# A two-block transformer on one core: the router's dependent chain runs without GpSimd beside it, and the overflow branch, the second gather, half of the list weights and the transposed lists move into later expert pairs

## The chip, the cores and the metric

The kernel runs on one core of a Trainium2 chip. A core has TensorE (matrix multiplies; PE in the rows, its weight loads PEld), VectorE (DVE), ScalarE (ACT), GpSimd (POOL) and SyncE (SP), which here only issues transfers. Each engine works through its own list of instructions in order; they meet at semaphores. All five share 16 DMA engines, which bring weights from the large memory (HBM) into the on-chip memory. The metric is device time of one execution in microseconds, smaller is better.

## The reference, cut to what matters

The program is two blocks on 256 tokens of width 1024. The change touches the mixture of experts that ends each of the two layers of the first block:

```python
def grouped_moe(x, router_w, router_bias, w_gate, w_up, w_down):
    scores = softmax(x @ router_w)                       # 16 experts in 4 groups
    biased = scores + router_bias
    # the best group by the sum of its two best biased scores; in it, the two best experts
    weights = sel / sum(sel)                             # of the two chosen scores
    combine = sum(one_hot(expert_idx, 16) * weights[..., None], axis=1)
    y = 0
    for e in range(16):
        he = silu(x @ w_gate[e]) * (x @ w_up[e])         # 1024 -> 512
        y = y + combine[:, e:e+1] * (he @ w_down[e])     # 512 -> 1024
    return y
x = layer_norm(ALPHA * x + grouped_moe(x), g, b)
```

Everything is float32, so one layer's experts hold 96 MB of weights in units of 1 MiB (1.049 MB): 16 experts by three matrices of 2 MiB.

## The kernel before, in words

The tokens stand as two tiles of 128 rows (index t). Ahead of a layer's experts, `add_ln_router` finishes a projection, adds it to the residual, normalizes it to `tt` and multiplies it with the router's weights, so that the logits `lg` come from TensorE while the second token tile is still being normalized. `zh` and `zl` are `tt` split in a rounded high part and the rest (`split`), as the operands of the gathers.

`route` then runs a chain of some forty small VectorE instructions (128x32 and smaller): softmax with an exact exponential, ranks, chosen groups, the selection `esel`, and, after five small matmuls that count positions (`pos`, `tot`), the position of each token in its expert's list (`posm`). Each expert has 64 slots. `Pm[h]` is a 0/1 matrix from tokens to slots for half h of the experts (h = 0: pairs 0 to 3; h = 1: pairs 4 to 7); `comb` holds the weights of the chosen experts. `ofint` says whether an expert got more than 64 tokens; if so, `overflow` does the rest in a branch on every engine. In the profiled run no engine enters it. `gather_half(h, ks)` multiplies `zh`, `zl` with `Pm[h]` and lets ScalarE put the result into the tiles `xg`, the experts' inputs.

`moe` goes over eight pairs of experts, two experts side by side in the 128 columns. Pair p: gate matmuls (`first(p, "gate")`, out `pg`), the transposed hidden state of the pair before, one half of the scatter of the pair before that (`back`, out `sct`), up matmuls (`pu`), silu and product (`gated`), the other half of the scatter, and the down matmuls of the pair before (`down`, out `po`). A pair takes 12 units of weights, 4 for each matrix. In pair 0 stand also the second gather, the weights of the lists turned to slots (`pc`, copied to `cg`), and the transposed lists `PT` (`PmT`), which the scatters need.

The weights of the whole program are one list, `order`; `Stream` loads it in that order from SyncE's queue. How far ahead it may load is the number of places that `W.spare` names by kind: `w` (tiles that elsewhere hold split weights), `big`, `x`, `q`, besides three `raw` tiles. A place is free again when TensorE has read its unit; SyncE waits for that in order, unit by unit. A transfer also waits for the transfer eight before it. The kernel is written in program order by hand (nothing reorders it). `ada_go` and `ada_end` put small pieces of the second block's modulation between.

In SyncE's list the end of the branch carries waits for all eight of its transfer semaphores: where they hold on the way past as well, every transfer issued before must have landed ere the next is issued. The other engines' lists carry there a wait for their own earlier work.

Of the kernel before, what the change touches and what calls it, by code (L numbers as in the profile page):

```python
# [213 lines left out]
def _build(nc, tc, A, out, ctx, order, plan):  # L214
# [266 lines left out]
    def add_ln_router(l, x_old, wname, xh, xl, nm):  # L481
# [32 lines left out]

        def rest():
            unit(1)
            for t in range(2):
                G.tensor_sub(zl[:, t], tt[:, t], zh[:, t].bitcast(F32))
            for t in range(2):
                for i, op in enumerate((OP.mult, OP.add)):  # L520
                    G.tensor_tensor(tt[:, t], tt[:, t], gb[:, i], op=op)

# [481 lines left out]
    def route(l, x):  # L1004

        tt, zh, zl, lg, rest = x
# [70 lines left out]
        def weights():  # L1077
            comb, cd = sm(32, "comb"), sm(2, "cd")
            V.tensor_tensor(comb, sc, eself, op=OP.mult)
            V.tensor_reduce(cd, r3(comb), axis=AX, op=OP.add)  # L1080
            V.reciprocal(cd, cd)
            V.tensor_tensor(r3(comb), r3(comb), b16(cd), op=OP.mult)
            return comb
# [11 lines left out]
        gather_half(0, range(8))  # L1095
        return xg, gather_half, Pm, comb, tt

# [50 lines left out]

    def beyond(l, pair, half, px, first, tt, zh, zl, P2, PT2, x2, o2, h2, ps, p, ps_, cg2):

        V.tensor_scalar_add(ps_, px[:, :2], -float(first))
        for t in range(2):
            V.tensor_scalar(P2[:, t], iota, ps_[:, t:t + 1], None, op0=OP.is_equal)
        f2 = x2[:, 0].rearrange("p (k n) -> p k n", k=8)
        for k in range(8):
# [29 lines left out]
        for nh in range(2):  # L1185
            c = slice(nh * 512, nh * 512 + 512)
            split(o2[:, 0, c], o2[:, 1, c], ps[2 + nh])
        for t in range(2):
            for nh in range(2):
                c = slice(nh * 512, nh * 512 + 512)  # L1190
                for i in range(2):
                    T.matmul(ps[nh], PT2[:, t], o2[:, i, c], start=i == 0, stop=i == 1)
                V.tensor_add(tt[:, t, c], tt[:, t, c], ps[nh])

    def moe(l, x, hooks):

# [30 lines left out]

        W.spare.update(big=1)
        for p in range(9):
            if p == 4:  # L1230
                W.spare["big"] = 3
# [5 lines left out]
            if p == 0:  # L1237
                gather_half(1, range(4), "BB")
                pc = mm([128, 128], "pc", "B")
                for q in range(8):  # L1240
                    for t in range(2):
                        T.matmul(pc[:, 16 * q:16 * q + 16], Pm[q // 4][:, t, 128 * (q % 4):128 * (q % 4) + 128].bitcast(F32),
                                 comb[:, 16 * t:16 * t + 16], start=t == 0, stop=t == 1)
                cg = cp.tile([128, 8], F32, name=f"cg{l}")
                for s in range(2):
                    V.tensor_copy(cg[64 * s:64 * s + 64], pc[64 * s:64 * s + 64, s:s + 127:18])
            else:
# [940 lines left out]
```

## Time and profile before

| | |
|---|---|
| time, three runs | 1975.96, 1968.2, 1970.99 us (median 1970.99) |
| the profiled execution | 1969.34 us, span from the first to the last instruction 1967.5 us |
| TensorE busy | 1839.5 us, 93% |
| VectorE / ScalarE / GpSimd busy | 984.3 / 706.3 / 392.3 us |
| transfers | 424.23 MB, mean 216 GB/s over the span |

TensorE's busy share is high everywhere, since matmuls overlap and their ends are modelled; it does not say that TensorE sets the time. The two expert stages lie at about 238 to 478 us and 696 to 938 us. In most of each the transfer rate stands at 422 GB/s.

### The profile page before, as it was taken

Reading aid. Unit: us, or ns where it says so; the run is one execution under the profiler, and the core shown is the slowest. Engines: PE = TensorE matmul, PEld = TensorE weight load, DVE = VectorE, ACT = ScalarE, POOL = GpSimd, SP = SyncE. Lnnn points to the kernel's source line nnn. Section 1 sums busy time; section 2 is a strip of 40 time slices with the busy share of each in tenths; the row PEclk is TensorE's granted clock in tenths of the full one; section 3 lists DMA queues with packets and bytes.
Section 4 is the critical chain, followed back from the end, with each engine's and each line's share of the span. In section 5 each row is a group of like instructions: output and inputs, shape, how many; then the busy total and the mean of one; then the engine's idle time right before and its main releaser. Section 6 shows DMA issues by size and latency. Waiting matters only on the chain.

```text
span 1967.5 us, 25607 instructions
## 1 busy us (share of the span) xinstructions
PE 1839.5 (93%) x10038; PEld 1332.9 (68%) x10038; DVE 984.3 (50%) x1717; ACT 706.3 (36%) x1214; POOL 392.3 (20%) x604
## 2 busy tenths in 40 slices
PE   8999699999999789999889989899999998999999
PEld 6888443334788553333678877688888886669998
DVE  6884601113785611112755666734353446756665
ACT  6654220002454331111454553522222225545442
POOL 0012200003334300020565673200000005410000
PEclk9999799999999889999999999999999999899999
DMA  7555679999756759999621221423333422455552
GB/s 260 203 207 201 235 278 421 422 423 423 285 193 219 273 198 408 422 422 423 249 108 66 86 65 65 135 102 130 105 129 107 136 87 65 181 220 197 186 181 106
DMA packets 81300, 424.23 MB, mean 216 GB/s; under 512 B 9376, under 2 KB 9824, under 8 KB 48656
## 3 DMA queue, kind: packets, MB, share of 16 engines
q1 hardware_dynamic: 78480, 409.66, 55.3%
q0 software_dynamic: 2688, 12.81, 1.8%
q8 instruction: 83, 1.36, 0.3%
q14 instruction: 49, 0.40, 0.1%
HBM read 421.35 MB, written 1.08 MB: 215 GB/s over the span
## 4 chain that ended last, share of the span: by engine, by line
PE 42%; DMA 8%; DVE 8%; ACT 3%; POOL 2%; issue 1%; ACTq 0%; DVEq 0%; POOLq 0%; SPq 0%
PE fg L1686 3%; PE fu L1687 3%; PE fu L1686 3%; PE fg L1687 3%; PE fu L1688 3%; PE fg L1688 3%; PE fd L339 3%; PE fd L340 3%; PE fd L341 3%; DMA spare<-up 3%; DMA spare<-gate 2%; DMA raw<-down 2%; DMA spare<-down 2%; PE qkvp L339 1%; PE qkvp L340 1%
## 5 line engine op out<-in xcount | busy, mean ns | idle before, releaser
L253 ACT CAST wh<-raw 128x1024 fp32r<-128x1024 f32 (+1 forms) x256 | 256.8, 1048 | 138.2 <-PE fd L341 90.6
L254 DVE TENSOR_TENSOR wl<-raw,wh 128x1024 fp32r<-128x1024 f32 (+1 forms) x197 | 242.8, 1266 | 82.2 <-ACT wh L253 81.9
L254 POOL TENSOR_TENSOR wl<-raw,wh 128x1024 fp32r<-128x1024 f32 x59 | 150.9, 2568 | 301.5 <-ACT wh L253 283.2
L1687 PE MATMUL fg<-f,wh 128*128 128x256 f32 (+1 forms) x360 | 120.6, 335 | 2.6 <-DVE f L1419 2.4
L1686 PE MATMUL fg<-f,wh 128*128 128x256 f32 (+1 forms) x360 | 121.1, 336 | 1.6 <-DVE f L1418 1.4
L1686 PE MATMUL fu<-f,wh 128*128 128x256 f32 (+1 forms) x360 | 120.5, 335 | 0.0
L1687 PE MATMUL fu<-f,wh 128*128 128x256 f32 (+1 forms) x360 | 120.5, 335 | 0.0
L1688 PE MATMUL fu<-f,wl 128*128 128x256 f32 (+1 forms) x360 | 120.4, 334 | 0.0
L1688 PE MATMUL fg<-f,wl 128*128 128x256 f32 (+1 forms) x360 | 120.0, 333 | 0.0
L339 PE MATMUL qkvp<-wh,h 128*128 128x256 f32 x384 | 112.8, 294 | 0.1
L340 PE MATMUL qkvp<-wl,h 128*128 128x256 f32 x384 | 109.1, 284 | 1.8 <-POOL wl L254 1.8
L1705 DVE TENSOR_TENSOR fsg<-fu,fsg 128x512 f32<-128x512 f32 (+1 forms) x44 | 24.5, 558 | 171.1 <-PE fu L1688 169.2
L341 PE MATMUL qkvp<-wh,h 128*128 128x256 f32 x384 | 108.9, 284 | 0.0
L1209 PE MATMUL pg<-spare,xg 128*64 128x512 f32 x376 | 96.6, 599 | 7.9 <-DMA spare<-gate 7.9
L1209 PE MATMUL pu<-spare,xg 128*64 128x512 f32 x400 | 101.0, 616 | 2.1 <-DMA spare<-up 1.9
L339 PE MATMUL fd<-wh,hid 128*128 128x512 f32 x264 | 103.0, 390 | 0.0
L340 PE MATMUL fd<-wl,hid 128*128 128x512 f32 x264 | 102.8, 389 | 0.0
L341 PE MATMUL fd<-wh,hid 128*128 128x512 f32 x264 | 102.7, 389 | 0.0
L1220 PE MATMUL po<-spare,hT 128*64 128x512 f32 x392 | 99.7, 600 | 1.5 <-DMA spare<-down 1.4
L253 ACT CAST oh<-po 128x512 fp32r<-128x512 f32 x32 | 18.8, 586 | 228.1 <-PE po L1220 228.1
L253 ACT CAST hid<-fsg 128x512 fp32r<-128x512 f32 (+1 forms) x44 | 22.6, 513 | 183.5 <-DVE fsg L1705 183.5
L1109 DVE SCALAR_TENSOR_TENSOR hm<-pu,cg,sg 128x512 f32<-128x512 f32 x16 | 12.0, 751 | 144.9 <-PE pu L1209 114.3
(666 smaller groups left out, 4313.2 us busy)
## 6 DMA issues: line engine op xcount, KB each, us to landing
spare<-up SPq DMA_DIRECT2D x90, 512.0 KB, 12.3
spare<-down SPq DMA_DIRECT2D x90, 512.0 KB, 9.9
raw<-gu SPq DMA_DIRECT2D x42, 1024.0 KB, 4.9
raw<-ada SPq DMA_DIRECT2D x34, 1024.0 KB, 4.9
spare<-gate SPq DMA_DIRECT2D x56, 512.0 KB, 9.8
raw<-dn SPq DMA_DIRECT2D x22, 1024.0 KB, 4.8
spare<-gate SPq DMA_DIRECT2D x19, 1024.0 KB, 13.5
raw<-gate SPq DMA_DIRECT2D x17, 1024.0 KB, 11.1
```

Of the source, the lines that this page charges most:

```text
L253: (H.tensor_copy if H else S.copy)(hi, src)
L254: E.tensor_sub(lo, src, hi.bitcast(F32))
L339: T.matmul(ps, sh, mh, start=start, stop=False)
L340: T.matmul(ps, sh, ml, start=False, stop=False)
L341: T.matmul(ps, sl, mh, start=False, stop=stop_)
L1109: V.scalar_tensor_tensor(hm, pu, cgc, sg, op0=OP.mult, op1=OP.mult)
L1209: T.matmul(ps[64 * s:64 * s + 64], xg[h][k // 4][:, k % 4, 128 * b + 64 * s:128 * b + 64 * s + 64], w[s][:, kk * 512:kk * 512 + 512], star ...
L1220: T.matmul(po[nh][64 * s:64 * s + 64], hT[:, k, 64 * s:64 * s + 64], w[s][:, nh * 512:nh * 512 + 512], start=k == 0, stop=k == 3)
L1686: T.matmul(ps[:, cs], hi[:, c], h_, start=k == 0, stop=False)
L1687: T.matmul(ps[:, cs], hi[:, c], l_, start=False, stop=False)
L1688: T.matmul(ps[:, cs], lo[:, c], h_, start=False, stop=k == 7)
L1705: V.tensor_tensor(sg[:, :n], pss[1][:, :n], sg[:, :n], op=OP.mult)
```

## The change

In `add_ln_router` the two GpSimd instructions that make `zl` are parted: that of tile 0 goes ahead, beside the projection; that of tile 1 goes to VectorE, where it stands between `esel` and the reading of `pos`. The four GpSimd instructions that multiply `tt` by the gain and add the bias go to VectorE, two into pair 0 and two into pair 1 (`affine`). `route` no longer holds the overflow branch; it stands in pair 4. `Pm[1]` is written after the list weights. The second gather goes from pair 0 to pairs 2 and 3, the weights of its half and its transposed lists to pair 3, the transposed lists of the first half to pair 1. Since the second half's two `xg` tiles are taken only in pair 2, `W.spare` has two `big` places from the start of `route` (none there before), one from pair 1 and three from pair 5 (before: one from pair 0, three from pair 4).

```diff
@@ add_ln_router
-        def rest():
-            unit(1)
-            for t in range(2):
-                G.tensor_sub(zl[:, t], tt[:, t], zh[:, t].bitcast(F32))
-            for t in range(2):
-                for i, op in enumerate((OP.mult, OP.add)):
-                    G.tensor_tensor(tt[:, t], tt[:, t], gb[:, i], op=op)
+        def low(t, E):
+            E.tensor_sub(zl[:, t], tt[:, t], zh[:, t].bitcast(F32))
+
+        def affine(t):
+            for i, op in enumerate((OP.mult, OP.add)):
+                V.tensor_tensor(tt[:, t], tt[:, t], gb[:, i], op=op)
...
         unit(0)
+        low(0, G)
         tm_half(pss, (1,), xh, xl, hs[3:], 6, 8)
...
-        return tt, zh, zl, lg, rest
+        unit(1)
+        return tt, zh, zl, lg, lambda: low(1, V), affine
@@ route
-        W.spare.update(w=5, x=2)
+        W.spare.update(w=5, x=2, big=2)
...
-        rest()
...
         tri, one = trio[:, 0], trio[:, 1]
+        low()
         T.matmul(pos[:, :16], tri, esel[:, :16], start=True, stop=True)
...
-        ada_end()
...
-        overflow(l, ofint, pm, weights, tt, zh, zl)
-        comb = weights()
-        xg = [[big([128, 4, 512], F32, "xg") for _ in range(2)] for _ in range(2)]
+        listed(0)
+        comb, cd = sm(32, "comb"), sm(2, "cd")
...
+        listed(1)
+        xg = [[big([128, 4, 512], F32, "xg") for _ in range(2)], []]
@@ moe
-        W.spare.update(big=1)
         for p in range(9):
-            if p == 4:
+            if p == 1:
+                W.spare["big"] = 1
+            if p == 5:
                 W.spare["big"] = 3
...
             if p == 0:
-                gather_half(1, range(4), "BB")
-                pc = mm([128, 128], "pc", "B")
...
+                gains(0)
...
             if p == 0:
-                gather_half(1, range(4, 8), "BB")
-                for h in range(2):
-                    for t in range(2):
-                        ps = tp([128, 4, 128])
-                        for i in range(4):
-                            T.transpose(ps[:, i], Pm[h][:, t, i * 128:i * 128 + 128].bitcast(F32), ident)
-                        S.copy(PT[h][:, :, t], ps)
+                ada_end()
+                affine(0)
+            if p == 1:
+                affine(1)
+                lists_T(0)
+            if p in (2, 3):
+                gather_half(1, range(4 * p - 8, 4 * p - 4), "BB")
+            if p == 3:
+                gains(1)
+                lists_T(1)
             if p > 1:
                 back(p - 2, 1)
+            if p == 4:
+                beyond_lists()
```

How the order on the engines moves, in layer 0. First GpSimd around the router: `zl` is the low part, `ln_0tt` the normalized tile, `ofint` the flag of the branch. Before:

```order
L254 TENSOR_TENSOR wl<-raw,wh 128x1024
L518 TENSOR_TENSOR zl<-ln_0tt,zh 128x1024 x2
L521 TENSOR_TENSOR ln_0tt<-ln_0tt,ln_0gb 128x1024 x4
L1131 TENSOR_LOAD ofint_2154
L1132 COMPARE_AND_BRANCH
```

Now:

```order
L254 TENSOR_TENSOR wl<-raw,wh 128x1024
L516 TENSOR_TENSOR zl<-ln_0tt,zh 128x1024
L1131 TENSOR_LOAD ofint_2154
L1132 COMPARE_AND_BRANCH
L1141 DMA lists_80<-both 128x8x8
```

Five of the six GpSimd instructions are gone from this place. On VectorE, from the selection on, it was:

```order
L1052 TENSOR_TENSOR esel<-sel,gsel 128x32
L1064 TENSOR_REDUCE ofi<-tot 128x1
L1065 TENSOR_SCALAR ofint_2154<-ofi 128x1
L1067 SCALAR_TENSOR_TENSOR posm<-pos,esel 128x32
L584 TENSOR_REDUCE ada_78<-adat 128x2x4
L585 TENSOR_TENSOR ada_78<-ada_78,prm 128x2x4
L1073 TENSOR_TENSOR Pm<-cst,posm 128x512 x4
L1131 TENSOR_LOAD ofint_2154
L1132 COMPARE_AND_BRANCH
```

and is now:

```order
L1052 TENSOR_TENSOR esel<-sel,gsel 128x32
L516 TENSOR_TENSOR zl<-ln_0tt,zh 128x1024
L1065 TENSOR_REDUCE ofi<-tot 128x1
L1066 TENSOR_SCALAR ofint_2154<-ofi 128x1
L1068 SCALAR_TENSOR_TENSOR posm<-pos,esel 128x32
L1074 TENSOR_TENSOR Pm<-cst,posm 128x512 x2
L1080 TENSOR_TENSOR comb<-rsc,esel 128x32
L1081 TENSOR_REDUCE cd<-comb 128x2
L1082 RECIPROCAL cd<-cd 128x2
L1083 TENSOR_TENSOR comb<-comb,cd 128x32
L1074 TENSOR_TENSOR Pm<-cst,posm 128x512 x2
```

The first half's `Pm` stands two instructions after `posm` instead of four behind two of the modulation, and one `zl` has come in ahead of `ofi`.

SyncE's queue from the first expert weights of layer 0 to the branch, before (an `x2` or `x8` of 128x1024 is half a unit each, 128x2048 a whole one):

```order
L294 DMA raw<-gate 128x2048
L291 DMA spare<-gate 128x1024 x6
L291 DMA spare<-up 128x1024 x8
L294 DMA raw<-gate 128x2048 x2
L291 DMA spare<-gate 128x1024 x2
L1131 TENSOR_LOAD ofint_2154
L1131 ISA x2
L1132 COMPARE_AND_BRANCH
```

The same place now:

```order
L294 DMA raw<-gate 128x2048
L291 DMA spare<-gate 128x1024 x6
L291 DMA spare<-up 128x1024 x4
L294 DMA spare<-up 128x2048 x2
L291 DMA spare<-gate 128x1024 x4
L294 DMA raw<-gate 128x2048 x2
L291 DMA spare<-up 128x1024 x2
L294 DMA raw<-up 128x2048
L291 DMA spare<-up 128x1024 x4
```

Eleven units stood ahead of the branch; now thirteen stand ahead of the first one that waits for an expert's matmul (`raw<-up`), and the branch stands in pair 4.

TensorE in pairs 0 and 1 of layer 0, from the gate matmuls of pair 0, before (`gat` is the second gather):

```order
L1209 MATMUL pg<-spare,xg 64x512 x12
L1000 MATMUL gat<-Pm,zh 128x512 x2
L1000 MATMUL gat<-Pm,zl 128x512 x2
...
L1242 MATMUL pc<-comb,Pm 128x16 x16
L1209 MATMUL pu<-spare,xg 64x512 x16
L1000 MATMUL gat<-Pm,zh 128x512 x2
...
L1260 MATMUL tp<-cst,Pm 128x128 x16
L1209 MATMUL pg<-raw,xg 64x512 x8
```

Now:

```order
L1208 MATMUL pg<-spare,xg 64x512 x12
L1232 MATMUL pc<-comb,Pm 128x16 x8
L1208 MATMUL pu<-spare,xg 64x512 x16
L581 MATMUL adat<-cst,adar 128x128 x4
L1208 MATMUL pg<-spare,xg 64x512 x8
L1208 MATMUL pg<-raw,xg 64x512 x8
L1101 MATMUL tp<-cst,hm 128x128 x4
L1208 MATMUL pu<-spare,xg 64x512 x4
L1208 MATMUL pu<-raw,xg 64x512 x4
L1208 MATMUL pu<-spare,xg 64x512 x8
L1243 MATMUL tp<-cst,Pm 128x128 x8
```

Pair 0 now holds 8 small `pc` matmuls and four transposes beside its own work; the 32 gather matmuls are in pairs 2 and 3.

## Rows read from the trace of the kernel before

**Rows 1.** Windows: engines' busy us (count), PEclk, DMA share, GB/s.

```profile
227.00:295.00 68.00, 58.07 (x267) 31.18 (x269) 9.76 (x32) 18.76 (x25) 1.10 (x1) 0.86 0.61 217
346.00:470.00 124.00, 114.20 (x454) 39.24 (x453) 22.29 (x34) 12.28 (x22) 2.59 (x3) 1.00 1.02 422
685.00:745.00 60.00, 50.71 (x235) 28.81 (x237) 9.68 (x31) 20.04 (x26) 2.38 (x2) 0.85 0.59 202
```

**Rows 2.** Timeline of TensorE, last waits for weights of each layer.

```profile
476.07 1.93 PE L1220 MATMUL po<-spare,hT 128*64 128x512 f32 x6 [0.19 <-DMA spare<-down]
923.10 1.94 PE L1220 MATMUL po<-raw,hT 128*64 128x512 f32 x8 [0.52 <-DMA raw<-down]
```

**Rows 3.** Groups by line on VectorE and GpSimd, router of layer 0.

```profile
L991 DVE SCALAR_TENSOR_TENSOR exp<-exp,exr 128x32 f32<-128x32 f32 x6 | 5.3, 880 | 0.2
L993 DVE SCALAR_TENSOR_TENSOR re<-exp,exs 128x32 f32<-128x32 f32 x1 | 2.3, 2294 | 0.0
L585 DVE TENSOR_TENSOR ada<-ada,prm 128x8 f32<-128x8 f32 x1 | 2.1, 2089 | 0.0
L1022 DVE TENSOR_TENSOR rsc<-re,rden 128x32 f32<-128x32 f32 x1 | 1.8, 1840 | 0.0
L988 DVE SCALAR_TENSOR_TENSOR exr<-exk,exr 128x32 f32<-128x32 f32 x1 | 0.2, 193 | 0.0
L521 POOL TENSOR_TENSOR ln_0tt<-ln_0tt,ln_0gb 128x1024 f32<-128x1024 f32 x4 | 9.4, 2356 | 0.2
L518 POOL TENSOR_TENSOR zl<-ln_0tt,zh 128x1024 fp32r<-128x1024 f32 x2 | 4.7, 2360 | 21.5 <-ACT zh L513 21.5
```

**Rows 4.** Timeline, end of the router's chain, layer 0 and layer 1.

```profile
219.47 1.94 PE L569 MATMUL ada<-spare,csil 128*32 128x512 f32 x8
...
231.19 0.19 DVE L1052 TENSOR_TENSOR esel<-sel,gsel 128x32 fp32r<-128x32 f32 x1
...
232.99 0.18 DVE L1067 SCALAR_TENSOR_TENSOR posm<-pos,esel 128x32 f32<-128x32 f32 x1
...
233.98 2.49 DVE L1073 TENSOR_TENSOR Pm<-cst,posm 128x512 fp32r<-128x512 f32 x4
...
238.34 1.19 PE L1000 MATMUL gat<-Pm,zh 128*128 128x512 f32 x2 [4.70 <-PEq L1132]
...
691.66 0.18 DVE L1067 SCALAR_TENSOR_TENSOR posm<-pos,esel 128x32 f32<-128x32 f32 x1
```

**Rows 5.** Chain of work that ended last, pair 0 of layer 1.

```profile
696.02 9.37 PE gat L1000 x32
705.40 7.02 PE pg L1209 x32
...
716.27 3.48 PE pc L1242 x32
...
728.46 3.89 PE gat L1000 x16
...
734.83 7.02 PE pg L1209 x32
```

**Rows 6.** Windows around the routers, and the first refill of layer 0.

```profile
227.00:238.00 11.00, 2.20 (x9) 1.80 (x9) 7.93 (x28) 1.28 (x1) 1.10 (x1) 0.50 0.03 6
250.00:252.00 2.00, 2.00 (x12) 0.62 (x10) 0.00 (x0) 0.00 (x0) 0.00 (x0) 1.00 0.55 86
685.00:696.00 11.00, 2.20 (x9) 1.81 (x10) 8.47 (x28) 1.28 (x1) 2.27 (x2) 0.50 0.02 7
```

**Rows 7.** Timeline of TensorE: gate matmuls of pairs 2 and 3, layer 1.

```profile
756.15 1.89 PE L1209 MATMUL pg<-raw,xg 128*64 128x512 f32 x8
...
779.69 5.32 PE L1209 MATMUL pg<-spare,xg 128*64 128x512 f32 x24
```

**Rows 8.** Instructions of the branch line: min/median/max ns, both layers.

```profile
L1132 PEldq COMPARE_BRANCH  x2: 3512/3880/4248, 233.7 to 692.2; - x2
```

**Rows 9.** DMA issues: KB each, median us from issue to landing.

```profile
spare<-up SPq DMA_DIRECT2D x90, 512.0 KB, 12.3
```

More of the change, by code (lines that the diff above doesn't have):

```diff
@@ L1004, in route @@
     def route(l, x):
-        tt, zh, zl, lg, rest = x
-        W.spare.update(w=5, x=2)
+        tt, zh, zl, lg, low, affine = x
+        W.spare.update(w=5, x=2, big=2)
         W.whole = 16
@@ L1067, in route, with listed @@
         V.scalar_tensor_tensor(pm, pos, 1.0, eself, op0=OP.add, op1=OP.mult)
-        ada_end()
         Pm = [q4([128, 2, 512], F32R, "Pm") for _ in range(2)]
-        for h in range(2):
+        def listed(h):
             for t in range(2):
@@ L1075, in route @@
                                 pm[:, e0:e0 + 8][:, :, None].to_broadcast([128, 8, SLOTS]), op=OP.is_equal)
[L1077 to L1083, printed above, removed]
-        overflow(l, ofint, pm, weights, tt, zh, zl)
-        comb = weights()
-        xg = [[big([128, 4, 512], F32, "xg") for _ in range(2)] for _ in range(2)]
+        listed(0)
+        comb, cd = sm(32, "comb"), sm(2, "cd")
+        V.tensor_tensor(comb, sc, eself, op=OP.mult)
+        V.tensor_reduce(cd, r3(comb), axis=AX, op=OP.add)
+        V.reciprocal(cd, cd)
+        V.tensor_tensor(r3(comb), r3(comb), b16(cd), op=OP.mult)
+        listed(1)
+        xg = [[big([128, 4, 512], F32, "xg") for _ in range(2)], []]
         def gather_half(h, ks, tags="AB"):
+            if not xg[h]:
+                xg[h] += [big([128, 4, 512], F32, "xg") for _ in range(2)]
             for k in ks:
@@ L1095, in route @@
         gather_half(0, range(8))
-        return xg, gather_half, Pm, comb, tt
+        return xg, gather_half, Pm, comb, tt, affine, lambda: overflow(l, ofint, pm, comb, tt, zh, zl)
     def hidden_T(hm):
@@ L1125, in scatter, with overflow @@
             V.tensor_add(tt[:, t, c], tt[:, t, c], ps)
-    def overflow(l, ofint, pm, weights, tt, zh, zl):
+    def overflow(l, ofint, pm, comb, tt, zh, zl):
         if plan:
@@ L1132, in overflow @@
         with tc.If(v0 > 0):
-            comb = weights()
             both, P2, PT2 = s2([128, 16, 4], F32, "both"), s2([128, 2, 128], F32R, "P2"), s2([128, 2, 128], F32R, "PT2")
-            x2, o2, h2 = big([128, 2, 1024], F32, "x2"), big([128, 2, 1024], F32R, "o2"), big([128, 3, 512], F32, "h2")
+            x2, h2 = big([128, 2, 1024], F32, "x2"), big([128, 3, 512], F32, "h2")
+            o2 = [q4([128, 1024], F32R, "o2") for _ in range(2)]
             ps = [mm([128, 512], "pg"), mm([128, 512], "pu")] + [mm([128, 512], f"po{nh}", "B") for nh in range(2)]
@@ L1153, in beyond @@
             V.tensor_scalar(P2[:, t], iota, ps_[:, t:t + 1], None, op0=OP.is_equal)
-        f2 = x2[:, 0].rearrange("p (k n) -> p k n", k=8)
+        f2, w = x2[:, 0].rearrange("p (k n) -> p k n", k=8), x2[:, 1]
         for k in range(8):
@@ L1162, in beyond @@
         S.copy(PT2, p[:, :2])
-        w = x2[:, 1]
         def chunk(nm, c):
@@ L1186, in beyond @@
             c = slice(nh * 512, nh * 512 + 512)
-            split(o2[:, 0, c], o2[:, 1, c], ps[2 + nh])
+            split(o2[0][:, c], o2[1][:, c], ps[2 + nh])
         for t in range(2):
@@ L1191, in beyond @@
                 for i in range(2):
-                    T.matmul(ps[nh], PT2[:, t], o2[:, i, c], start=i == 0, stop=i == 1)
+                    T.matmul(ps[nh], PT2[:, t], o2[i][:, c], start=i == 0, stop=i == 1)
                 V.tensor_add(tt[:, t, c], tt[:, t, c], ps[nh])
     def moe(l, x, hooks):
-        xg, gather_half, Pm, comb, tt = route(l, x)
-        PT = [q4([128, 4, 2, 128], F32R, "PmT") for _ in range(2)]
+        xg, gather_half, Pm, comb, tt, affine, beyond_lists = route(l, x)
+        PT = [None, None]
+        cg = cp.tile([128, 8], F32, name=f"cg{l}")
         hm, hT, o = {}, {}, {}
@@ L1226, in back, with gains, lists_T @@
             scatter(*o[p], PT[p // 4][:, p % 4, t], tt, t, *tags)
-        W.spare.update(big=1)
+        def gains(h):
+            pc = mm([128, 64], "pc", "B")
+            for q in range(4):
+                for t in range(2):
+                    T.matmul(pc[:, 16 * q:16 * q + 16], Pm[h][:, t, 128 * q:128 * q + 128].bitcast(F32),
+                             comb[:, 16 * t:16 * t + 16], start=t == 0, stop=t == 1)
+            for s in range(2):
+                V.tensor_copy(cg[64 * s:64 * s + 64, 4 * h:4 * h + 4],
+                              pc[64 * s:64 * s + 64, 8 * h + s:8 * h + s + 55:18])
+        def lists_T(h):
+            PT[h] = q4([128, 4, 2, 128], F32R, "PmT")
+            for t in range(2):
+                ps = tp([128, 4, 128])
+                for i in range(4):
+                    T.transpose(ps[:, i], Pm[h][:, t, i * 128:i * 128 + 128].bitcast(F32), ident)
+                S.copy(PT[h][:, :, t], ps)
         for p in range(9):
-            if p == 4:
+            if p == 1:
+                W.spare["big"] = 1
+            if p == 5:
                 W.spare["big"] = 3
@@ L1237, in moe @@
             if p == 0:
-                gather_half(1, range(4), "BB")
-                pc = mm([128, 128], "pc", "B")
-                for q in range(8):
-                    for t in range(2):
[L1242 to L1246, printed above, removed]
+                gains(0)
             else:
@@ L1254, in moe @@
             if p == 0:
-                gather_half(1, range(4, 8), "BB")
-                for h in range(2):
-                    for t in range(2):
-                        ps = tp([128, 4, 128])
-                        for i in range(4):
-                            T.transpose(ps[:, i], Pm[h][:, t, i * 128:i * 128 + 128].bitcast(F32), ident)
-                        S.copy(PT[h][:, :, t], ps)
+                ada_end()
[8 more added lines that the diff above has]
+                lists_T(1)
             if p > 1:
                 back(p - 2, 1)
+            if p == 4:
+                beyond_lists()
             if p in hooks:
```

## The prediction

> **What bounds the kernel now.** I read the transfer line of the page first, then windows over the two expert stages, then TensorE's timeline in them, and last the router in groups and in order of time. In a window from 346 to 470 us (columns: length; busy time and count of PE, PEld, DVE, ACT, POOL; granted clock; DMA share; GB/s) the 16 DMA engines are fully busy at 422 GB/s while TensorE, busy for 114.20 of 124 us, has gaps [rows 1]. The gaps end with a weight transfer's landing: so it stands in TensorE's row at 476.07 us in layer 0 and at 923.10 us in layer 1 [rows 2]. There the weight stream sets the pace, and an expert stage ends as early as 96 units of 1.049 MB have come in. At 422 GB/s a unit takes 2.49 us, and nothing in this change alters that rate or the number of units.
>
> What can change is the time in which the stream stands still. From 227 to 295 us it moves only 217 GB/s, from 685 to 745 us 202 GB/s [rows 1]. Against 422 that is 68 x (1 - 217/422) = 33.0 us lost in layer 0 and 60 x (1 - 202/422) = 31.3 us in layer 1. Its first part is seen in the windows 227 to 238 and 685 to 696 us, at 6 and 7 GB/s [rows 6]: all places are full and no expert matmul has freed one, because TensorE waits for the router's chain. The rest is pair 0: the second gather, `pc` and the transposes stand between the gate and up matmuls and free no place.
>
> **The change, part by part.**
>
> *Chain without GpSimd.* VectorE's small instructions take about 0.19 us, as L988 does. In the same chain six of L991 take 5.3 us, L993 2.3, L1022 1.84, L585 2.09 [rows 3]; at 0.19 each they would take 1.15, 0.19, 0.19 and 0.17. The excess is 4.1 + 2.1 + 1.65 + 1.9 = 9.8 us, and it falls on the stretch in which GpSimd runs `zl` and the four `ln_0tt` instructions of 2.36 us each [rows 3]. These five go. I take the whole 9.8 us; the lower bound is nothing (if the delay were not GpSimd's), but five held instructions against five GpSimd ones leave little room for it. VectorE then reaches `esel` at 231.19 - 9.8 = 221.4 us; TensorE's earlier matmuls end at 219.47 + 1.94 = 221.4 [rows 4], so the five count matmuls are just not delayed.
>
> The one `zl` that VectorE takes over is issued between `esel` and `ofi`. `esel` ends at 231.38 and `posm` starts at 232.99 [rows 4]; 1.6 us are spent mostly on TensorE's counting. The instruction is as large as GpSimd's of 2.36 us, which is the upper price; I count it at nothing, with up to 1 us beyond the cover.
>
> *Gather start.* After `posm` it needs two of the four `Pm` (2.49 / 2 = 1.25 us) and no branch. `posm` would end at 232.99 + 0.18 - 9.8 = 223.4 and the gather start at about 224.8 us, against 238.34: 13.5 us earlier. In layer 1, 691.66 + 0.18 - 9.8 + 1.4 = 683.4 against 696.02: 12.6 us [rows 4, 5]. [...] I keep the 9.4 us that the gather took from there [rows 5].
>
> *Pair 0.* It loses the second gather (two pieces of 3.89), half of `pc` (3.48 / 2 = 1.7) and the transposes (734.83 - 728.46 - 3.89 = 2.5) [rows 5]: 12 us a layer, not removed but put into pairs 1 to 3, where TensorE would otherwise come to wait for weights.
>
> *The stream.* Two more places of 1 MiB are filled during the chain: 2 x 2.49 = 5.0 us more of full transfer, so that in layer 0 it stands still from 232 instead of 227 us and in layer 1 from 690 instead of 685. It starts again when the first gate unit is read: gather start + 9.4 + one unit's matmuls (a quarter of 7.02 = 1.8 us) [rows 5], which is 236.0 and 694.6 us. The first 2 us after a restart carry 86 GB/s, which loses 1.6 us [rows 6]. From there TensorE frees a unit every 1.8 us, faster than 2.49, and pair 0 has no long gap left: I count no further loss before pair 4.
>
> *The branch in pair 4.* Past it, SyncE may have to see everything landed before it issues again. If so, the stream runs empty once: a restart at 1.6 us and some 0.9 us of issuing, 2.5 us a layer. Bounds: 0, if it need not wait; the landing time of a unit's half, 12.3 us [rows 9], if SyncE's next instructions come only behind the weights. I take 2.5, nearest to the restart row. TensorE itself stood 3.5 and 4.2 us at its branch [rows 8], in a stretch where the DMA engines were idle; here I take the 4.2.
>
> [...]
>
> Sum, layer 0: 33.0 - (236.0 - 232) - 1.6 - 2.5 = 24.9 us. Layer 1: 31.3 - (694.6 - 690) - 1.6 - 2.5 = 22.6. Together 47.
>
> *Can TensorE keep up?* From its first gate matmul it has: pair 0 16, pair 1 21 + 1, pairs 2 to 7 six times 779.69 - 756.15 = 23.5 [rows 7], the moved 10.5, the branch 4.2, the last scatter and down 10: about 204 us (16 and 21 from the pieces of 7.02, the last 10 from 7.02 and a scatter). Starting at 234.2 it would be through at 438, while the stream ends at 476 - 25 = 451; in layer 1 at 693 + 204 + 4 = 901 against the last unit's about 933 - 23 = 910 (923.10 plus four units). So 10 us of slack cover the moved work and the branch; if they did not, those would be paid in full.
>
> *The affine on VectorE* (four instructions, at most 2.36 each by GpSimd's row) lies in pairs 0 and 1, where VectorE is busy for 9.76 of 68 us [rows 1]; nothing waits for `tt` before the first scatter in pair 2. Its GpSimd work was 9.4 us off the path but for the chain.
>
> What follows a stage depends on its last scatter, so I let the gain carry through whole. The profiled execution took 1969.3 us, 1.65 less than the median of the three runs: 1969.3 - 47 = 1922.3, or 1924 in terms of the median.
>
> **Rivals.**
>
> *Only the chain counts (B).* If TensorE, not the stream, ends the stage, the 12 us of pair 0 come back in pairs 1 to 3, and 13.5 + 12.6 = 26 us remain: 1945. For it: the slack is only 10 us of 204, and every delay in the middle eats of it. Against: the gaps for weights before [rows 1, 2].
>
> *The branch under load (C).* If SyncE's and TensorE's next instructions arrive only after some 12.3 us, the median landing in a busy queue [rows 9], the stream idles some 10 us more a layer: 47 - 20 = 27 us, 1944. No row yet tells it from 4.2 us. [...]
>
> *Slower (D).* The drain decides: SyncE stands at the branch until all has landed, frees come unheeded, and TensorE then starves behind an empty queue. It would have to cost more than 2.5 + 47 / 2 = 26 us a layer, over two landings of 12.3 one after the other (transfers, then instructions), to undo the gain; at three landings, 37 us, it gives 47 - 69 = 22 us more than before, 1993.
>
> *No gain from the chain (E).* If VectorE's long instructions are slow for another reason and the places are not free in time, only the added places and the missing branch ahead of the gather count, and the branch in pair 4 takes that back: about 1969.
>
> **How the numbers follow.** Likeliest, 0.62: both gains, 1924, itself 1912 to 1938 (slack of the sum: clock at the gather, 0 to 6 us for a drain, 1 us for `zl`). B 0.17 and C 0.09: 1944, between 1935 and 1952. More than forecast, under 1912 (no drain, gather at full clock): 0.05. D 0.03, E 0.04. The range 1910 to 1950 leaves out the ends, about 2 in 10. A measurement here tells about 0.5%, 10 us, from no change: faster 0.92, same 0.05, slower 0.03.
>
> **What would show it.** After: L991, L993, L1022 and L585 at 0.19 us in the router; gather starts 12 to 14 us earlier after the end of the projection; the window without transfers about 4 us long; 422 GB/s from there to the stage's end, with one short dip in pair 4; TensorE's last row in each stage still ended by a weight transfer. Wrong: TensorE without waits for weights in pairs 5 to 7 (B), a TensorE or SyncE stall over 8 us at the branch (C), or transfers below 422 GB/s in pairs 1 to 3, where places would not be freed in the order in which SyncE waits for them.

## The result and the profile after

The changed kernel takes 1927.97 us in the median of four runs (1925.9 to 1929.8), the kernel before 1973.1 in four runs (1968.2 to 1975.96): a ratio of 0.9773, 95% interval 0.9749 to 0.9798. The forecast was 1924, its range 1910 to 1950. The profiled execution took 1929.8 us with a span of 1928.0, against 1967.5 before; what follows reads these two.

First VectorE's groups of the router in layer 0 (busy time, mean ns of one, idle time before), which answer to [rows 3]; most line numbers have moved by one:

```profile
L516 DVE TENSOR_TENSOR zl<-ln_0tt,zh 128x1024 fp32r<-128x1024 f32 x1 | 1.2, 1216 | 0.0
L992 DVE SCALAR_TENSOR_TENSOR exp<-exp,exr 128x32 f32<-128x32 f32 x6 | 1.2, 193 | 0.2
...
L586 DVE TENSOR_TENSOR ada<-ada,prm 128x8 f32<-128x8 f32 x2 | 0.3, 168 | 0.1
...
L994 DVE SCALAR_TENSOR_TENSOR re<-exp,exs 128x32 f32<-128x32 f32 x1 | 0.2, 193 | 0.0
...
L1022 DVE TENSOR_TENSOR rsc<-re,rden 128x32 f32<-128x32 f32 x1 | 0.2, 192 | 0.0
```

The four long groups of before are gone. In order of time, the chain from its first maximum (`rmx`) to the gather, then `rmx` of before in both layers and of now in layer 1:

```profile
216.42 0.19 DVE L1014 TENSOR_REDUCE rmx<-rlg 128x2 f32<-128x32 f32 x1
...
224.02 0.19 DVE L1052 TENSOR_TENSOR esel<-sel,gsel 128x32 fp32r<-128x32 f32 x1
224.13 1.22 DVE L516 TENSOR_TENSOR zl<-ln_0tt,zh 128x1024 fp32r<-128x1024 f32 x1
225.54 0.17 DVE L1065 TENSOR_REDUCE ofi<-tot 128x1 f32<-128x16 f32 x1 [0.19 <-PE tot L1061]
...
225.82 0.18 DVE L1068 SCALAR_TENSOR_TENSOR posm<-pos,esel 128x32 f32<-128x32 f32 x1
226.10 1.29 DVE L1074 TENSOR_TENSOR Pm<-cst,posm 128x512 fp32r<-128x512 f32 x2
```

```profile
213.79 0.19 DVE L1014 TENSOR_REDUCE rmx<-rlg 128x2 f32<-128x32 f32 x1
...
672.47 0.19 DVE L1014 TENSOR_REDUCE rmx<-rlg 128x2 f32<-128x32 f32 x1
```

```profile
648.34 0.19 DVE L1014 TENSOR_REDUCE rmx<-rlg 128x2 f32<-128x32 f32 x1
```

The gather starts on TensorE:

```profile
226.94 1.30 PE L1001 MATMUL gat<-Pm,zh 128*128 128x512 f32 x2 [1.43 <-DVE Pm L1074]
...
658.57 1.30 PE L1001 MATMUL gat<-Pm,zh 128*128 128x512 f32 x2 [1.67 <-DVE Pm L1074]
```

From `rmx` to `esel` it is 7.6 us, before, where `rmx` starts at 213.79, 231.19 - 213.79 = 17.4 [rows 4]: 9.8 less. From `rmx` to the gather it is 10.5 instead of 24.55 us, and in layer 1 (`rmx` at 648.34, before at 672.47) 10.2 instead of 23.55: 14.0 and 13.3 us less. `ofi` still waits 0.19 us for TensorE behind `zl`, so that instruction is covered. The program stands 2.6 us later at `rmx` of layer 0 than before. That delay is older than the router: GpSimd's last `wl` of the projection ahead of it starts at 192.65 us, before at 190.01.

The stream in 2 us steps around the restart, and in 10 us steps in pair 4 (the last column is GB/s):

```profile
230.00:232.00 2.00, 2.00 (x8) 1.59 (x8) 0.00 (x0) 0.94 (x2) 0.00 (x0) 0.79 0.92 375
232.00:234.00 2.00, 2.00 (x11) 1.64 (x10) 0.00 (x0) 1.74 (x3) 0.00 (x0) 1.00 0.27 107
234.00:236.00 2.00, 2.00 (x11) 1.61 (x9) 0.00 (x0) 1.75 (x3) 0.00 (x0) 1.00 0.00 0
236.00:238.00 2.00, 2.00 (x10) 0.63 (x10) 0.00 (x0) 1.85 (x3) 0.00 (x0) 1.00 0.00 0
238.00:240.00 2.00, 2.00 (x12) 0.72 (x10) 0.00 (x0) 0.46 (x1) 0.00 (x0) 1.00 0.52 66
240.00:242.00 2.00, 2.00 (x12) 0.67 (x10) 0.00 (x0) 0.00 (x0) 0.00 (x0) 1.00 0.89 369
242.00:244.00 2.00, 2.00 (x15) 0.90 (x11) 0.00 (x0) 0.56 (x1) 0.00 (x0) 1.00 0.98 313
```

```profile
360.00:370.00 10.00, 10.00 (x50) 4.08 (x48) 1.42 (x3) 1.09 (x2) 0.00 (x0) 1.00 0.84 343
370.00:380.00 10.00, 9.58 (x39) 3.28 (x36) 1.94 (x3) 0.00 (x0) 0.00 (x0) 1.00 0.82 269
380.00:390.00 10.00, 8.52 (x28) 2.01 (x28) 1.38 (x2) 1.17 (x2) 0.00 (x0) 1.00 1.02 424
...
800.00:810.00 10.00, 7.61 (x26) 2.15 (x22) 0.61 (x2) 1.28 (x4) 0.00 (x0) 0.88 0.52 176
```

The first dip is the standing ahead of the restart, the second the branch, which is not short. Its instructions in pair 4 of both layers (ns: least, median, most; first and last start), and SyncE's wait at it in layer 0 (total, times, longest):

```profile
L1132 PEldq COMPARE_BRANCH  x2: 5797/5837/5877, 345.5 to 777.8; - x2
...
L1132 SPq COMPARE_BRANCH  x2: 50/52/53, 356.9 to 793.7; - x2
```

```profile
SPq L1132 <- SPq L1132: 13.0, 1, 13.0
```

TensorE stood 5.8 us at it, SyncE 13.0 us (356.9 to 369.9) in layer 0 and 10 us in layer 1. TensorE's last waits for a weight transfer in each stage, which answer to [rows 2]:

```profile
457.69 1.93 PE L1219 MATMUL po<-spare,hT 128*64 128x512 f32 x6 [0.17 <-DMA spare<-down]
...
882.52 1.94 PE L1219 MATMUL po<-spare,hT 128*64 128x512 f32 x8 [0.52 <-DMA spare<-down]
```

476.07 - 457.69 = 18.4 us earlier in layer 0 (21.0 without the 2.6 us of late start), 923.10 - 882.52 = 40.6 by the end of layer 1's; at the program's end 39.5 are left.

**An account.** If the stream sets the pace, a stretch costs its length x (1 - rate/422). I took this in every run from 10 us ahead of `rmx` to 120 us behind it (the restart) and from there on 100 us more (pair 4), in both layers. The restart windows of before, and all four of the kernel after, read:

```profile
203.79:333.79 130.00, 110.58 (x537) 53.50 (x538) 36.57 (x89) 30.15 (x42) 14.06 (x6) 0.89 0.79 302
...
662.47:792.47 130.00, 113.00 (x543) 54.15 (x544) 37.41 (x94) 33.01 (x45) 16.25 (x10) 0.89 0.82 310
```

```profile
206.42:336.42 130.00, 124.67 (x610) 57.92 (x610) 36.34 (x101) 30.15 (x43) 2.35 (x1) 0.95 0.96 389
336.42:436.42 100.00, 92.07 (x380) 32.13 (x378) 15.11 (x23) 7.85 (x14) 0.00 (x0) 1.00 0.98 399
638.34:768.34 130.00, 123.12 (x606) 57.98 (x606) 37.10 (x106) 33.00 (x46) 3.99 (x4) 0.96 0.96 387
768.34:868.34 100.00, 89.33 (x364) 31.49 (x362) 15.27 (x24) 10.63 (x22) 12.27 (x29) 0.95 0.97 394
```

| kernel | GB/s in the four windows | transfer lost, us | less after's | span less after's | median less after's |
|---|---|---|---|---|---|
| before | 302, 422, 310, 423 | 37.0 + 0 + 34.5 + 0 = 71 | +38 | +39.5 | +45.1 |
| after | 389, 399, 387, 394 | 10.2 + 5.5 + 10.8 + 6.6 = 33 | | | |
| before_chain | 329, 422, 341, 423 | 53 | +20 | +21.8 | +24.2 |
| pool_back | 357, 400, 358, 400 | 50 | +17 | +17.6 | +21.1 |
| pair0_nobig | 292, 400, 294, 398 | 90 | +57 | +59.1 | +57.4 |
| pair0_affine_early | 351, 402, 352, 398 | 54 | +21 | +24.2 | +21.9 |
| no_big | 373, 400, 374, 399 | 41 | +8 | +4.8 | +7.8 |
| q_places2 | 398, 399, 396, 401 | 26 | -7 | -6.9 | -4.0 |
| q_places3 | 406, 401, 407, 399 | 20 | -13 | -7.6 | -8.6 |
| no_branch | 390, 422, 389, 422 | 20 | -13 | -13.9 | -12.4 |
| branch_route | 371, 422, 373, 422 | 31 | -2 | -2.2 | +1.0 |
| branch_gap | 379, 422, 376, 422 | 27 | -6 | -0.7 | +0.5 |
| branch_gap_q2 | 389, 422, 388, 422 | 21 | -12 | -9.6 | -6.0 |
| branch_p7 | 387, 422, 389, 422 | 21 | -12 | +2.2 | +2.4 |

The account and the span are of the same execution. In ten of the thirteen rows they agree within 4 us; the others are q_places3 (5), branch_gap (5) and branch_p7 (14). Medians differ from the spans by up to 6 us more: the profiled execution of before (1969.34) lay 3.8 us under its median, that of after 1.8 above, and an interval of a ratio is some 4 us to either side. The medians were also taken on several chips, where that of before lay between 1970.8 and 1973.1. A difference under 5 us between two medians says little here.

The account holds where the stream sets the pace, and there alone. From `rmx` to the last wait for weights layer 0 took 262.3 us before and takes 241.3 now, 21.0 less (the account says 21.3); layer 1 took 250.6 and takes 234.2, 16.5 less (the account 17.1). That 38 comes so near to the whole 39.5 is luck in part: 5.8 us more were gained between the layers (196.4 us from the last wait of layer 0 to `rmx` of layer 1, now 190.7), 2.6 were lost at the late start and 1.1 behind layer 1. Between the layers TensorE waits once for VectorE's `h1l` in the next projection; the rows are of before, of after and of branch_gap:

```profile
524.00 1.94 PE L569 MATMUL ada<-spare,csil 128*32 128x512 f32 x8 [3.47 <-DVE h1l L254]
```

```profile
502.66 1.06 PE L570 MATMUL ada<-raw,csil 128*32 128x512 f32 x8 [0.76 <-DVE h1l L254]
```

```profile
499.56 1.06 PE L570 MATMUL ada<-spare,csil 128*32 128x512 f32 x8 [3.48 <-DVE h1l L254]
```

In before the granted clock stands at 0.50 from 524 to 528 us behind that wait; now it stays at 1.00. before_chain and branch_gap_q2 wait as before does (3.46 and 3.47 us), no other kernel longer than 2.7. Why VectorE is later there in some kernels is not parted, with one trace of each.

### The profile page after: what moved, and what is told of

Same layout as the page of the kernel before. It is cut to its first block, busy times and chain, and to the rows that moved or that the text cites. A ratio compares the mean times of both kernels' runs of the same rounds, so it can differ in the third digit from the quotient of the medians.

```text
span 1928.0 us, 25653 instructions
## 1 busy us (share of the span) xinstructions
PE 1824.9 (95%) x10038; PEld 1333.6 (69%) x10038; DVE 975.5 (51%) x1731; ACT 703.8 (37%) x1212; POOL 369.4 (19%) x594
## 4 chain that ended last, share of the span: by engine, by line
PE 62%; DMA 10%; DVE 9%; ACT 4%; POOL 2%; issue 1%; SPq 0%; ACTq 0%; DVEq 0%; POOLq 0%
PE pu L1208 4%; DMA spare<-down 4%; PE pg L1208 4%; PE fg L1702 3%; PE fu L1703 3%; PE fu L1704 3%; PE fu L1702 3%; PE fg L1703 3%; PE fg L1704 3%; PE fd L340 3%; PE fd L341 3%; PE fd L339 3%; PE po L1219 3%; DMA spare<-gate 3%; PE gat L1001 2%; DMA spare<-up 2%
## 5 line engine op out<-in xcount | busy, mean ns | idle before, releaser
L253 ACT CAST wh<-raw 128x1024 fp32r<-128x1024 f32 (+1 forms) x248 | 248.7, 1048 | 131.7 <-PE fd L341 90.5
L254 POOL TENSOR_TENSOR wl<-raw,wh 128x1024 fp32r<-128x1024 f32 x56 | 143.7, 2580 | 252.9 <-ACT wh L253 246.0
L1219 PE MATMUL po<-spare,hT 128*64 128x512 f32 x456 | 111.4, 598 | 6.2 <-DMA spare<-down 2.2
L1208 PE MATMUL pu<-spare,xg 128*64 128x512 f32 x360 | 90.8, 607 | 6.8 <-DMA spare<-up 6.7
L1208 PE MATMUL pg<-spare,xg 128*64 128x512 f32 x360 | 87.3, 596 | 4.0 <-DMA spare<-gate 3.9
L1219 PEld LDWEIGHTS po<-spare,hT 128*64 128x64 f32 x456 | 35.9, 136 | 73.8 <-issue 48.5
## 6 DMA issues: line engine op xcount, KB each, us to landing
spare<-up SPq DMA_DIRECT2D x80, 512.0 KB, 12.4
raw<-gate SPq DMA_DIRECT2D x19, 1024.0 KB, 12.3
```

What stands on the lines that cost most here:

```text
L253: (H.tensor_copy if H else S.copy)(hi, src)
L254: E.tensor_sub(lo, src, hi.bitcast(F32))
L1208: T.matmul(ps[64 * s:64 * s + 64], xg[h][k // 4][:, k % 4, 128 * b + 64 * s:128 * b + 64 * s + 64], w[s][:, kk * 512:kk * 512 + 512], star ...
L1219: T.matmul(po[nh][64 * s:64 * s + 64], hT[:, k, 64 * s:64 * s + 64], w[s][:, nh * 512:nh * 512 + 512], start=k == 0, stop=k == 3)
```

## The experiments

All are cut from the kernel before or after; ratios are to the kernel before. The branch is entered in none of them.

**before_chain.** Only the chain's part of the change.

```diff
-        rest()
...
+        unit(0); low(0, G)                   # add_ln_router, as changed
...
+        low()                                # between esel and pos, on VectorE
...
         comb = weights()
+        affine(0); affine(1)                 # on VectorE
```

> The kernel before with one part of the change alone: no GpSimd work beside the router's chain (low part of tile 0 earlier on GpSimd, that of tile 1 and the affine on VectorE, the affine behind the list weights). Branch, second gather, lists and places stay as before; were the branch entered, what it adds would be scaled too. Theory 1 (what counts is the time in which the weight stream stands still, and each term adds): 9.8 us a layer, 1973.1 - 19.6 = 1953.5. Theory 2 (the chain carries all of the gain that was measured, the moved work comes back on TensorE): 1973.1 - 45 = 1928. Theory 3 (the long VectorE instructions have another reason): 1973.

Measured 1952.18 us, 0.9903 (0.988 to 0.9925). Theory 1 holds; 2 and 3 fall. Less than half of the gain is the chain (20.2 of 45.1 us), and that part arrives whole.

**pool_back.** The other way round.

```diff
 def affine(t):
-    V.tensor_tensor(...)
+    G.tensor_tensor(...)
@@ route
+        low(); affine(0); affine(1)          # low on GpSimd as well
         mx, d, e, sc, bi = ...
```

> The changed kernel with the affine and the low part of tile 1 back on GpSimd at the start of the route, so that five GpSimd instructions of 2.36 us lie beside the chain again; the rest as changed. Theory 1: the nine to ten held VectorE instructions come back in number five to six a layer, some 2 us each, so the gather starts 9 to 10 us later and the time is 1928 + 19 = 1947. Theory 2 (the chain counts for everything): up to 1973. Theory 3 (another reason for the long instructions): 1928, and L992 stays at 0.19 to 0.25 us.

Measured 1949.06 us, 0.989 (0.9872 to 0.9909). VectorE's groups are those of [rows 3] again:

```profile
L992 DVE SCALAR_TENSOR_TENSOR exp<-exp,exr 128x32 f32<-128x32 f32 x6 | 5.3, 880 | 0.2
L994 DVE SCALAR_TENSOR_TENSOR re<-exp,exs 128x32 f32<-128x32 f32 x1 | 2.3, 2292 | 0.0
L586 DVE TENSOR_TENSOR ada<-ada,prm 128x8 f32<-128x8 f32 x2 | 2.3, 1128 | 0.1
L1025 DVE TENSOR_TENSOR rsc<-re,rden 128x32 f32<-128x32 f32 x1 | 1.8, 1840 | 0.0
```

Five GpSimd instructions, five held ones on VectorE, one each (two of the six L992). That the hold is GpSimd's doing is shown: 1.84 to 2.3 us for one beside GpSimd, 0.17 to 0.19 without. By what it holds them is not shown. All held ones of the chain have two tensor inputs; between them `rden`, a reduction, took 0.19 us, but so did `rbi`, which has two.

**no_branch.** `beyond_lists()` in pair 4 left out; tokens beyond 64 of a list would be lost, and there are none.

```diff
-            if p == 4:
-                beyond_lists()
```

> The changed kernel without the overflow branch; it leaves out the tokens beyond 64 of a list, of which there are none in this run. Theory 1, from the trace after (343 and 269 GB/s where 422 is the rate in layer 0, 176 and 398 in layer 1: 5.5 and 6.4 us of transfer lost): 1928 - 12 = 1916. Rival 1, the forecast's term of 2.5 us a layer: 1923. Rival 2, the branch is hidden by TensorE's slack: 1928. The dips in pair 4 should be gone, and TensorE's last row in the stage should still end with a weight transfer.

Measured 1915.58 us, 0.9716 (0.9696 to 0.9735). The branch costs 12.4 us, 6 a layer, as read from the dips.

**pair0_nobig.** Second gather, list weights and transposed lists back in pair 0.

```diff
-        W.spare.update(w=5, x=2, big=2)
+        W.spare.update(w=5, x=2)
@@ moe, p == 0
+                gather_half(1, range(4), "BB")
                 gains(0)
+                gains(1)
...
+                gather_half(1, range(4, 8), "BB")
+                lists_T(0); lists_T(1)
```

> The changed kernel with the second gather, the weights of both halves and the transposed lists back in pair 0, and with no big place before pair 1 (those tiles are then taken by the second gather); chain and branch as changed. Theory 1: pair 0 holds 12 us of matmuls again that free no place, and two units, 5.0 us, are not loaded ahead: 14 to 17 us a layer, 1928 + 31 = 1959. Theory 2 (TensorE sets the end of the stage, so the order of its work does not matter): 1928 to 1933. The window without transfers should begin 5 us earlier, and the rate between gate and up of pair 0 should fall far below 422 GB/s.

Measured 1985.35 us, 1.0063 (1.0043 to 1.0084): slower than before, 26 us beyond theory 1. SyncE's waits of layer 0 (215 to 345 us) say why:

```profile
SPq L294 <- DVE ln_0tt L520: 23.8, 1, 23.8
SPq L294 <- PE pg L1208: 15.2, 1, 15.2
```

The next load was to go into the buffer that holds gain and bias, and the affine that frees it now stood in pair 1, behind all that was in pair 0. SyncE's list is in order, so everything queued behind one place: from 270 to 286 us nothing was transferred. The edit had a fault of its own; the next run takes it away.

**pair0_affine_early.** The same, with the affine behind the list weights.

```diff
+        affine(0); affine(1)
         W.limit = 2
         W.load(len(order))
         gather_half(0, range(8))
```

> As pair0_nobig, but the four affine instructions stand on VectorE right behind the list weights instead of in pairs 0 and 1; were the branch entered, nothing changes. In pair0_nobig SyncE stood 23.8 us behind the affine of pair 1, because the tile of gain and bias kept the buffer of the one big place. Theory 1 (the stream's standing time adds up): without that wait the move to pair 0 costs 14 to 17 us a layer as I had it, 1928 + 31 = 1959. Theory 2 (the order of TensorE's work does not matter, only SyncE's wait cost something in pair0_nobig): 1928 to 1938. A third: the wait was not the cause, 1985 stays.

Measured 1949.85 us, 0.9893 (0.9866 to 0.992): 21.9 us above the changed kernel, not the 31 of theory 1 nor within theory 2's 10. The account gives 21, so the kind of loss is right, and I had sized it too large; the 12 and 5 us a layer do not simply add.

**no_big.** `big=2` in the route left out.

> The changed kernel with only the two big places of the route taken away (one big place from pair 1 on, as changed). Theory 1: two units, 5.0 us a layer, are not loaded while the stream would stand still, 1928 + 10 = 1938; the window without transfers begins 5 us earlier. Rival: TensorE's 10 us of slack or the later places make up for it, 1928 to 1931.

Measured 1935.72 us, 0.9836 (0.9809 to 0.9862): two places are worth 8 us, 3.9 a layer of the 5.0.

**branch_route.** The branch back ahead of the gather.

```diff
+        overflow(l, ofint, pm, comb, tt, zh, zl)
         W.limit = 2
         W.load(len(order))
         gather_half(0, range(8))
```

> The changed kernel with the overflow branch back in the route, right before the gather (were it entered, what it adds would be scaled by the affine that comes later). There the stream stands still anyway, so its drain costs nothing and TensorE's stall of some 3 us ahead of the gather counts: 1928 - 12 + 6 = 1922. Rival 1: the branch costs the same at either place, 1928. Rival 2: the stall ahead of the gather is longer now that TensorE has no 10 us to reach the branch, 6 us a layer and more: 1930.

Measured 1928.96 us, 0.9795 (0.977 to 0.9821): the same as in pair 4, which both rivals said; theory 1's 1922 falls. The stream did not stand still there yet: during TensorE's stalls of 6.0 and 5.8 us it moved 384 and 410 GB/s (224 to 230 and 657 to 663 us). TensorE ahead of the gather:

```profile
230.07 1.19 PE L1001 MATMUL gat<-Pm,zh 128*128 128x512 f32 x2 [7.55 <-PEq L1133]
```

It waits 7.55 us where the changed kernel waits 1.43 for `Pm`.

**branch_p7.** `if p == 7` instead of `if p == 4`.

> The changed kernel with the branch in pair 7 instead of pair 4, ahead of the down matmuls of pair 6. With 13 places all eight units that are left should have been issued by then, so SyncE's drain holds up only weights of the next stage; TensorE's stall of some 6 us is made up but for 1 to 2 us while it runs after the stream (0.55 us a unit over 8 units): 1928 - 12 + 3 = 1919. Rival 1: the drain costs the same there, 1928. Rival 2: the next stage's first weights come late by the drain and its beginning waits for them, 1924 to 1930.

Measured 1930.4 us, 0.9799 (0.9775 to 0.9823): rivals. The stream is whole in the four windows, but behind it TensorE is what is late:

```profile
437.29 1.67 PE L1219 MATMUL po<-raw,hT 128*64 128x512 f32 x3 [3.81 <-PEq L1132]
442.51 2.82 PE L1219 MATMUL po<-raw,hT 128*64 128x512 f32 x5 [3.55 <-issue]
```

A second gap of 3.55 us follows the first, and no wait for weights comes after these in the stage; SyncE stood 12.2 and 14.3 us at its branch. Against no_branch the way from `rmx` to the next stage's first matmul (`memk`) is 7.7 us longer in layer 0 (246.3 against 238.5), with no wait for weights behind the gaps, and from there to layer 1's `rmx` only 1.5 (188.7 against 187.1). So in layer 0 it is TensorE's lateness that costs, not the next stage's weights; behind layer 1's `rmx` 6.0 more are lost, and these were not parted.

**branch_gap.** The branch behind the first gather, the affine ahead of it, one big place in the route.

```diff
+        affine(0); affine(1)
         W.limit = 2
         W.load(len(order))
         gather_half(0, range(8))
+        overflow(l, ofint, pm, comb, tt, zh, zl)
```

> The changed kernel with the branch right behind the first gather, where the stream stands still, with the affine ahead of it behind the list weights, and with one big place in the route instead of two (the branch's own tiles need the other). If TensorE's stall at a branch depends on what the transfer queues carry, it is 3.4 to 4.2 us there, as in layer 1 of before_chain (3.39), and it delays the restart; nothing is lost to the drain. Saved 12.4 (as without the branch), lost 2 x 3.4 to 4.2 for the stall and 4 for the place (half of what no_big lost): 1926 to 1928. Rival: the stall is 5.8 us at any place, 1931.

Measured 1928.5 us, 0.9773 (0.9758 to 0.9788): the total is as expected, not the parts.

```profile
L1135 PEldq COMPARE_BRANCH  x2: 3312/3500/3688, 229.6 to 662.7; - x2
```

```profile
PE pg L1211 <- PEq L1135: 0.4, 1, 0.4
```

The stall is 3.3 and 3.7 us, and TensorE runs the gather's queued matmuls meanwhile (busy for all of 229 to 233 us), so that `pg` waits 0.4 us. By the account this should have brought 6 us. Between the layers 4.6 of them are taken back: from the first `memk` matmul to `rmx` of layer 1 it is 191.6 us against 187.0 in the changed kernel, with the wait of 3.48 us for `h1l` shown above. Whether the branch's place brings that wait about is open.

**q_places2 and q_places3.** One and two more places in the route, the second run with `q=3`:

```diff
-        W.spare.update(w=5, x=2, big=2)
+        W.spare.update(w=5, x=2, big=2, q=2)
...
             if p == 1:
-                W.spare["big"] = 1
+                W.spare.update(big=1, q=1)
```

> The changed kernel with one further place for weights in the route (q = 2 there, back to one from pair 1 on). Theory 1: one unit, 2.5 us a layer, 1928 - 5 = 1923. Rival 1 (the lists' matrices get their buffers late): 1928 or more. Rival 2 (the slow restart is the loss): 1927.

> The changed kernel with two further places for weights in the route (q = 3 there, back to one from pair 1 on); branch in pair 4 as changed. In the trace after, the stream stands still for about 4 us ahead of a layer's restart and comes back slowly: 8.9 and 9.4 us of transfer lost in the windows 210 to 340 and 650 to 760 us. Theory 1 (standing time is what costs, and a place is worth what it fills of it): two units, 5.0 us of transfer, of which the 4 us of standing are filled: 1928 - 8 = 1920. Rival 1: the matrices of the lists take their buffers from the same tiles and come late, so the gather starts later, 1928 or more. Rival 2: the loss is the slow restart, which stays: 1926 to 1928.

Measured 1924.0 us, 0.9763 (0.9748 to 0.9778), and 1919.39 us, 0.9724 (0.9709 to 0.9738). Both are theory 1's numbers within a microsecond. With `q=3` the stream in layer 0 no longer stands still:

```profile
234.00:236.00 2.00, 2.00 (x11) 1.59 (x9) 0.00 (x0) 1.75 (x3) 0.00 (x0) 1.00 1.00 412
236.00:238.00 2.00, 2.00 (x10) 0.63 (x10) 0.00 (x0) 1.86 (x3) 0.00 (x0) 1.00 0.73 293
238.00:240.00 2.00, 2.00 (x12) 0.72 (x10) 0.00 (x0) 0.45 (x1) 0.00 (x0) 1.00 0.48 115
```

This kernel has the lowest median of the complete ones, 8.6 us under the changed one; that of branch_gap_q2, 2.6 us above it, cannot be told from it.

**branch_gap_q2.** `branch_gap` with `q=2` in the route and `listed(1)` at the end of pair 0.

> As branch_gap, with one further place for weights in the route (q = 2 there, one from pair 1 on) and the matrix of the second half's lists written at the end of pair 0 instead of ahead of the gather, so that its tile is free for that. The number of places is that of the changed kernel again; the branch stands behind the first gather. In branch_gap TensorE's 3.3 us at the branch lay under gather matmuls already queued and it waited 0.36 us. Theory 1 (transfer lost is time): what is left is the standing time of the changed kernel without the branch's dip, 17 to 19 us of transfer lost, 1915 to 1918. By what branch_gap measured instead (no gain from the branch's place, 4 us for the place): 1924. Rival: something else in that layout takes back what the branch's place saves, 1928.

Measured 1921.97 us, 0.9747 (0.9729 to 0.9765). That lies between theory 1 (1915 to 1918) and the 1924 by branch_gap. The account says 12 us under the changed kernel, the span 9.6, the median 6.0; between the layers it takes 191.6 us, as branch_gap does. It is no better than `q=3` alone.

## Why the prediction came out right, step by step

**What bounds it.** Right. Each stage's last wait is still for weights, and the two stages became 37.5 us shorter, where the transfer lost in the windows says 38. Rival B (only the earlier gather counts, 26 us, 1944) falls by the 45.1 us, and by pair0_affine_early: the work put back into pair 0, with its two places, costs 21.9. Its sign, no waits for weights in pairs 5 to 7, stayed away. Rival E (no gain from the chain) falls by before_chain, D (slower) by the result.

**Chain.** 9.8 us a layer forecast, and found from `rmx` to `esel` in both layers, and pool_back brings the five held instructions back. `zl`, counted at nothing, takes 1.22 us under cover.

**Gather start.** 13.5 and 12.6 us forecast, 14.0 and 13.3 found. The gather kept its time in layer 0, 9.3 us; in layer 1 it took 10.2, the clock standing at 0.50 to 664 us.

**Pair 0 and places.** Ahead of pair 4 I forecast 33.0 - 5.6 = 27.4 us less lost in layer 0 and 31.3 - 6.2 = 25.1 in layer 1; the account gives 37.0 - 10.2 = 26.8 and 34.5 - 10.8 = 23.7. At the restart itself I was off by more: in layer 0 the stream stands 5.5 us by the steps of 232 to 238 us, where I had 4, and comes back over 6 us (66, 369, 313 GB/s, 2.5 us lost) rather than the 2 us of [rows 6] at 1.6. The longer windows of the account hold small losses before as well as after, which made up for most of it. In the sum of whether TensorE can keep up, the last 4 us in layer 1's 901 come from no row; without them the slack there is 13 us.

**The branch.** This term was mis-sized. I took 2.5 us a layer for the drain, nearest to the restart row; it is 5.5 and 6.6 in the windows and 6.2 by no_branch. No row shows the 0.9 us of issuing in it; in layer 0 the first packets came 1.0 to 1.5 us behind the issue. SyncE does wait for all that is outstanding (in layer 0 until 369.9 us, with no packet from 369.5 on), and then the transfers have to come up again: SyncE's next issue is at 370.5, after 14 us without one, and the rate is back at 374 us. The sign that I had named for rival C came, a stall over 8 us at the branch: SyncE stood 13.0 and 10.0 us, about the 12.3 us of a landing [rows 9]. C's price did not, 12.5 us a layer: what had been issued ran on meanwhile, at 418 GB/s from 350 to 360 us and 343 to 370. So I was some 3.7 us a layer short, and C 6.3 above. Nor was the dip short, as I had written. TensorE's stall, taken at 4.2, was 5.8, and TensorE had the slack for it: its later waits, in pairs 4 to 7, are for weights.

**Together.** The branch's 12.1 instead of 5.0 us and 2 us of the restart leave 38 where I had 47. The two medians lie 45.1 us apart, nearer to the forecast than the mechanism is, and that closeness is luck: the profiled execution of before lay 3.8 us under its median, that of after 1.8 above, and where those 5.6 us lie no trace shows. The 5.8 us between the layers, too, were in no term of mine.

## What to carry to other kernels

Where a stream of weights bounds a stage, price an edit by the transfer it loses (length x (1 - rate / full rate)) rather than by the busy time it moves; here that followed the span within 4 us in ten of thirteen cases. The account ends where the stream does: work put behind the last transfer (branch_p7, 7.7 us in layer 0) is paid on the engines, and 5 us between the stages can come or go unseen by it. So compare the stages themselves, not only the totals. And an untaken branch is no free instruction (here TensorE stood 5.8 us at it, SyncE 13.0 and 10.0): ask what each engine's queue must have finished at it, the one that issues transfers above all.

## What the runs showed of the hardware

TensorE's time at the untaken branch was 3.3 and 3.7 us at 6 GB/s (branch_gap, 229 to 233 and 662 to 666 us), 3.5 and 4.2 before [rows 8] at 14 (692.2 to 695.7 and 233.7 to 237.9 us), and 5.8 to 6.0 us at 384 to 422 GB/s (after, branch_route, branch_p7). The mean rate alone does not decide: before_chain has 5.8 and 3.4 us at 189 and 204 GB/s (224 to 230 and 674 to 678 us). ScalarE and VectorE pass it in 45 to 72 ns. Why TensorE stands there so long is not shown.

Instructions are in the traces as transfers in a queue of their own. In after from 349 to 350 us, and in branch_gap from 230 to 231 us (transfers, MB, share of 16 engines):

```profile
q8 instruction: 1, 0.02, 6.0%
```

```profile
q8 instruction: 1, 0.02, 8.0%
```

The first lies in a stall from 345.5 to 351.3 us, the second in one from 229.6 to 232.9; no_branch has none from 340 to 362 us. before_chain has one at 227 to 228 us, some 3 us into the longer stall, and one at 675 to 676, some 1 us into the shorter. Each of these stalls ends 1 to 3 us behind its transfer. That the transfer is TensorE's, and that it comes later because it stands among the weights, is not shown; the views do not name its engine.

When TensorE starved in layer 1 after the branch (busy for 0.01 us from 806 to 808 us), its granted clock stood at 0.50 from 808 to 816 us, and six `pu` matmuls at 813.02 us took 3.67 us, where six at 405.75 us took 1.93.
